# Seven block products for two more pairs of a feed-forward layer, with the input's block sums made two in a slot

## The chip, the cores and the metric

The kernel runs on one core of a Trainium2 chip. Its time is the device time of one execution in microseconds (us). TensorE (PE) does the matmuls, VectorE (DVE) and ScalarE (ACT) the elementwise work, GpSimd (POOL) a little more of it, and SyncE (SP) issues the DMAs. Each engine works through its own queue in order; they meet through semaphores.

## The reference

One transformer block on x of 512 tokens by 1024 features, in float32: a SwiGLU feed-forward, a token mixer (dilated attention and pooling), a second SwiGLU feed-forward and a last RMSNorm, each conditioned by shifts, scales and gates that come from a small vector c through w_ada. What matters here is the first feed-forward:

```python
def swiglu(u, w_in, w_out):
    a, b = jnp.split(u @ w_in, 2, axis=-1)
    return (jax.nn.silu(a) * b) @ w_out

u = modulate(rmsnorm(h, g_norm_ffn1[l]), sh1, sc1)
h = h + 0.5 * gt1 * swiglu(u, w_ffn1_in[l], w_ffn1_out[l])
```

The inner width D_FF is 2816, that is 22 tiles of 128 columns for a and 22 for b.

## The kernel before

**Layout and precision.** Everything is held with features on the 128 partitions and the 512 tokens along the free axis. A float32 product is made of three matmuls of rounded parts (fp32r): high weights by high input, high by low, low by high. So each weight chunk of 128 x 1024 (one DMA of 512 KB into one of three `raw` buffers) is first *split*: ScalarE rounds it into the ring `whi` (L280), VectorE subtracts that from the original into `wlo` (L292). The ring has place for seven chunks. `look(n)` splits the chunks up to n ahead of the one that PE takes next, as far as raw buffers are free, and the place where it is called in the program sets the place of the splits in the queues of ScalarE and VectorE. The normalised input u is held in the same way as UH and UL.

**Pairs and parts.** A pair j is tile j of a and of b; silu(a) * b of it is one 128-row tile of the second matmul's input, kept as high and low parts HI, HK. The 22 tiles are worked in five parts (`PARTS`): input matmuls for some pairs, then the output projection of one part, whose results are added into H, eight tiles of 128 features, by VectorE (L852). Before the projection of part 0 stand pairs 4 and 5 (pairs 0 to 3 belong to the start); before that of part 1 pairs 6 to 9; then four more pairs for each part.

**Plain pairs and duos.** A plain pair (`ffn_pair`) takes two weight chunks and 2 x 24 matmuls with 512 moving columns (L323 to L325). A *duo* does two pairs at once by Strassen's scheme in its form with few additions (Winograd's): the weights of two pairs (halves of the 1024 rows by 256 columns for a and 256 for b) and u (halves of the features by halves of the tokens) are cut into 2 x 2 blocks, and seven products of blocks replace eight. In `duo` they are numbered 0 to 6; each is 24 matmuls with 256 moving columns (`product`, L709 to L711), into three banks in the order A, B, A, C, A, B, A. Since A goes on accumulating, ScalarE must copy it out after products 0, 2 and 4, and the copies stand directly behind them in the program (L716): after product 0 A is copied into bank C, after product 2 into `u2`, after product 4 into `u3`; B is copied into `p5` after product 1.

The seven weight operands, in the order in which they are taken, come from the four loaded blocks r11, r12, r22, r21 as follows (`make`, L228, on VectorE):

```
0: r11        1: x0 = r12 - r11    2: x1 = r22 - x0    3: r21
4: r12 = r22 - r12 (in place)      5: r22              6: x0 = r21 - x1
```

Each is then split like a loaded chunk. x0 and x1 live in two of four big tiles X, which hold the blocks of u (a11, a12, a21, a22) until the sums are made; the other two become additional raw buffers once the first duo has begun.

**The sums of u's blocks** (`u_steps`) are made once: sums S0, S1, S2 on VectorE (L669) with a rounding by ScalarE (L675) and a low part by VectorE (L676), and one last difference whose split (L678, L679) comes behind product 0 of the first duo. These are seven steps in the list `todo`. `ffn` takes one step from it behind each of the eight adds into H in the projection of part 0, and the sums write over a11 and a21, where the weight differences go.

**Order around the change in the old kernel.** Pairs 4 and 5, projection of part 0 (with the sums), pairs 6 and 7 plain, duo 8 (pairs 8 and 9), projection of part 1, two duos, projection, and so on. The second feed-forward has the same parts, with its pairs 0 to 3 plain, and is not touched.

**Conditioning work.** Beside plain pairs and behind the adds into H of parts 1 to 3, `bg` does one step of the product of w_ada with c on VectorE (L346), each with a DMA of 512 KB. 24 such steps are left after part 0 and must be done by the end of part 3's projection.

Of the kernel before, what the change touches and what calls it, by code (L numbers as in the profile page):

```python
# [115 lines left out]

U_AT = (0, 16, 0)

PLAIN = {0: 8, 2: 4}
PARTS = ((0, 4), (4, 8), (8, 12), (12, 16), (16, 22))  # L120
NH = 6

# [14 lines left out]
class Kernel:  # L137
# [6 lines left out]
    def plan(self):  # L144
        (i1, o1), mix, (i2, o2) = chunk_widths()
        self.chunks = []
        for name, ws in (("wf1i", i1), ("wf1o", o1), ("wmix", mix), ("wf2i", i2), ("wf2o", o2)):
            off, rec = 0, []
            for w in ws:
                rec.append((name, off, w))  # L150
                off += P * w
            self.chunks.append(rec)
        f1i, f1o, mx, f2i, f2o = self.chunks


        self.loads, self.order, self.last = [], [], {}

        def plain(recs):
            for r in recs:
                n = len(self.loads)  # L160
                self.loads.append(r)
                self.last[n] = len(self.order)
                self.order.append((r[2], n, ("raw", n), None))

        def blocks(recs):
            n = len(self.loads)
            self.loads.extend(recs)
            r11, r12, r22, r21 = (("raw", n + i) for i in range(4))
            x0, x1 = ("x", 0), ("x", 1)
            for need, src, make in ((0, r11, None), (1, x0, (x0, r12, r11)), (2, x1, (x1, r22, x0)), (3, r21, None),  # L170
                                    (3, r12, (r12, r22, r12)), (3, r22, None), (3, x0, (x0, r21, x1))):
                for j, x in enumerate((r11, r12, r22, r21)):
                    if x == src or (make and x in make):
                        self.last[n + j] = len(self.order)
                self.order.append((D, n + need, src, make))

        def ffn(n, ins, outs, first):
            j, at = first, 0
            if first:
                plain(ins[:KT])  # L180
                at = KT
            for part, (k0, k1) in enumerate(PARTS):
                while j < pairs_before(n, part):
                    if j < PLAIN[n]:
                        plain(ins[at:at + 2])
                        j, at = j + 1, at + 2
                    else:
                        blocks(ins[at:at + 4])
                        j, at = j + 2, at + 4
                plain(outs[part * KT // 2:(part + 1) * KT // 2] if part + 1 < len(PARTS) else outs[-KT:])  # L190

        ffn(0, f1i, f1o, FIRST)
        base = len(self.order)
        plain(mx)
        ffn(2, f2i, f2o, 0)
        self.fetched = self.done = self.made = 0
        self.pos, self.held, self.retired, self.half = 0, None, [], None
        self.at, self.start, self.top = {}, {}, 0
        self.buf = {}
        self.units = {base + i: 2 * P for i in (4, 5)}  # L200
        self.units.update({base + i: T for i in range(16, 20)})
# [55 lines left out]
    def split_hi(self):  # L257

        held = max(self.pos - 1, 0) if self.held is None else self.held
        i = self.done  # L260
        if self.half or i == len(self.order):
            return False
        got = self.room(i, held)
        if got is None:
            assert i >= self.pos, "no room"
            return False
        self.start[i] = self.top
        self.at[i], self.top = got
        self.fetch(i)
        assert self.fetched > self.order[i][1], "no buffer"  # L270
        self.make(i)
        r = self.source(self.order[i][2])
        parts = []
        for o, c in self.at[i]:
            for x in self.pieces(i, self.order[i][0]):
                x = slice(max(x.start, c.start), min(x.stop, c.stop))
                if x.start < x.stop:
                    parts.append((slice(o + x.start - c.start, o + x.stop - c.start), x))
        for y, x in parts:
            self.nc.scalar.activation(self.hi[:, y], r[:, x], AF.Copy)  # L280
        if i + 1 < len(self.order) and self.order[i + 1][3] and self.order[i + 1][1] < self.fetched:
            self.make(i + 1)
        self.half = (r, parts)
        return True
# [529 lines left out]
    def ffn(self, n, j, last=None):  # L814
# [10 lines left out]
        for part, (k0, k1) in enumerate(PARTS):  # L825
            tail = part + 1 == len(PARTS)
            while j < pairs_before(n, part):
                if j < PLAIN[n]:
                    self.ffn_pair(j, beside)
                    j += 1  # L830
                else:
                    self.duo(j, last, tail and j + 2 == FT)
                    last = None
                    j += 2
            if n == 0:
                last = self.beside_out(part) or last
            nk = k1 - k0
            hk = [(self.HH[k % NH], self.HL[k % NH]) for k in range(k0, k1)]
            if not tail:
                for m in range(0, KT, 2):  # L840
                    self.look(4)
                    w = self.take()
                    bs = [self.nb(), self.nb()]

                    for ka, kb in ((0, nk - 1), (nk - 1, nk)) if m == 0 else ():
                        for i in range(2):
                            for k in range(ka, kb):
                                self.mm3(bs[i], *w[nk * i + k], *hk[k], k == 0, k == nk - 1)
                    for i, b in enumerate(bs):
                        for k in range(nk if m else 0):  # L850
                            self.mm3(b, *w[nk * i + k], *hk[k], k == 0, k == nk - 1)
                        v.scalar_tensor_tensor(self.H[m + i], b, gate[:, m + i:m + i + 1], self.H[m + i],  # L852
                                               op0=OP.mult, op1=OP.add)
                        if n == 0 and part:
                            self.bg()
                        if self.todo:
                            self.todo.pop(0)()
                    self.step()
                continue

            def ks(m):
                self.look(max(3, min(m + 2, 5)))
                return [(hi, lo, *hk[k]) for k, (hi, lo) in enumerate(self.take())]

            if n == 2:
                self.sums.close()
                op = self.f2.enter_context(self.tc.tile_pool(name="f2o", bufs=1))
                self.OO = op.tile([P, KT * T], F32, name="out").rearrange("p (m t) -> p m t", m=KT)
                self.O = [self.OO[:, m, :] for m in range(KT)]

            kl = [ks(0), ks(1)]
            bs = [self.nb(), self.nb()]
            for ka, kb in ((0, nk - 2), (nk - 2, nk)):
                for m in range(2):
                    for k in range(ka, kb):
                        self.mm3(bs[m], *kl[m][k], k == 0, k == nk - 1)
            for m in range(3 if n else 4):
                if m > 1:
                    bs.append(self.nb())
                    for k, x in enumerate(ks(m)):  # L880
                        self.mm3(bs[m], *x, k == 0, k == nk - 1)
                v.scalar_tensor_tensor(self.H[m], bs[m], gate[:, m:m + 1], self.H[m], op0=OP.mult, op1=OP.add)
                self.sumsq(m, self.H[m])
                if n == 2:
                    nc.scalar.activation(self.O[m], self.H[m], AF.Copy, scale=self.g(3)[:, m:m + 1])
                for _ in range(6):
                    if self.todo:
                        self.todo.pop(0)()
            if n:
                self.out_end((3, 4, 5, 6, 7), ks, gate)  # L890
            else:
                self.trig_spread()
                self.out_tail((4, 5, 6, 7), ks, gate, 1, lambda m: self.X[0][:, m % 2 * HT:])

    def beside_out(self, part):

        if part == 0:
# [4 lines left out]
            self.bg_fetch()  # L902
            self.sums = self.open_sums()
            self.todo, last = self.u_steps(0)
            return last
        if part == len(PARTS) - 1:
            assert self.ada_next == 48 and not self.adat, self.ada_next
# [637 lines left out]
```

## Time and profile before

| | |
|---|---|
| median of three runs | 1030.19 us (1028.4 to 1030.54) |
| the profiled execution | 1027.69 us, span of its instructions 1025.9 us |
| busy: TensorE, weight load, VectorE, ScalarE | 1010.4, 912.5, 750.4, 435.1 us |
| mean granted TensorE clock | 0.994 |
| HBM read | 135.82 MB |

Busy times are those of the one profiled execution. A matmul's row holds start and duration in the pipeline, so the durations of successive matmuls overlap; how long a stage takes on TensorE is read from the starts. A row in square brackets names what ended the idle time in front of an instruction. Lines (L...) are those of the old kernel; in the new one they are two to seven higher.

### The profile page before, as it was taken

The page shows a single profiled execution, that of the slowest core. Times are in us where ns is not written, and L with a number is a line of the kernel's source. Part 1 is how long each engine was busy: PE and PEld are TensorE (multiplying, and loading weights), DVE is VectorE, ACT ScalarE, POOL GpSimd, SP SyncE. Part 2 cuts the span into 40 slices and gives each one's busy share as a digit, 9 for nine tenths or more (in the row PEclk, how much of TensorE's full clock was granted, in tenths as well). Part 3 has the DMA queues.
Part 4 walks back from the last instruction along what each step waited for, and adds up shares of the span by engine and source line. Part 5 has one row for each costly group of instructions (what it writes and reads, how often), then busy time and mean ns, then how long its engine had stood idle before and what let it go on. Part 6 is the DMA issues. An engine that isn't in the chain of part 4 may idle for free.

```text
span 1025.9 us, 15526 instructions
## 1 busy us (share of the span) xinstructions
PE 1010.4 (98%) x6364; PEld 912.5 (89%) x6364; DVE 750.4 (73%) x1073; ACT 435.1 (42%) x638; POOL 37.7 (4%) x39
## 2 busy tenths in 40 slices
PE   8999999999999899999999999999999999999997
PEld 6888898989999899889988888898899899998997
DVE  7968779789786677779546777467787776676754
ACT  6443253525434452334324333454355344352553
POOL 0000000000000100006200000200000000000011
PEclk9999999999999989999999999999999999999998
DMA  9866456555523323222144774322344224241312
GB/s 337 276 213 226 129 200 206 164 165 168 182 72 117 105 78 100 66 79 77 40 176 164 267 248 141 100 67 64 101 148 140 83 96 152 83 142 45 109 35 83
DMA packets 43113, 139.60 MB, mean 136 GB/s; under 512 B 4897, under 2 KB 8225, under 8 KB 43042
## 3 DMA queue, kind: packets, MB, share of 16 engines
q1 hardware_dynamic: 42034, 137.82, 41.1%
q8 instruction: 50, 0.82, 0.3%
q10 hardware_dynamic: 1008, 0.79, 0.2%
q14 instruction: 21, 0.17, 0.1%
HBM read 135.82 MB, written 2.77 MB: 135 GB/s over the span
## 4 chain that ended last, share of the span: by engine, by line
PE 95%; DVE 2%; ACT 1%; issue 1%; DMA 0%; ACTq 0%; DVEq 0%
PE bank L323 17%; PE bank L324 17%; PE bank L325 17%; PE bank L709 10%; PE bank L711 10%; PE bank L710 10%; PE bank L1475 2%; PE bank L1477 1%; PE bank L1479 1%; PE bank L1074 1%; PE bank L1253 1%; PE bank L1254 1%; PE bank L1255 1%; PE bank L1022 1%; PE bank L1051 1%
## 5 line engine op out<-in xcount | busy, mean ns | idle before, releaser
L292 DVE TENSOR_TENSOR wlo<-raw,whi 128x1024 fp32r<-128x1024 f32 (+2 forms) x151 | 176.9, 1175 | 75.6 <-ACT whi L280 75.3
L280 ACT ACTIVATE whi<-raw 128x1024 fp32r<-128x1024 f32 (+2 forms) x151 | 150.4, 1003 | 41.8 <-DVE raw L228 39.9
L323 PE MATMUL bank<-UH,whi 128*128 128x512 f32 (+1 forms) x432 | 159.0, 368 | 0.0
L324 PE MATMUL bank<-UL,whi 128*128 128x512 f32 (+1 forms) x432 | 154.9, 359 | 0.2 <-DVE UL L451 0.2
L325 PE MATMUL bank<-UH,wlo 128*128 128x512 f32 (+1 forms) x432 | 154.9, 358 | 0.0
L323 PE MATMUL bank<-HI,whi 128*128 128x512 f32 (+1 forms) x406 | 147.6, 364 | 0.0
L324 PE MATMUL bank<-HK,whi 128*128 128x512 f32 (+1 forms) x406 | 147.1, 362 | 0.0
L325 PE MATMUL bank<-HI,wlo 128*128 128x512 f32 (+1 forms) x406 | 147.0, 362 | 0.0
L709 PE MATMUL bank<-UH,whi 128*128 128x256 f32 x512 | 141.6, 277 | 0.0
L710 PE MATMUL bank<-UL,whi 128*128 128x256 f32 x512 | 141.6, 277 | 0.0
L711 PE MATMUL bank<-UH,wlo 128*128 128x256 f32 x512 | 141.6, 277 | 0.0
L292 DVE TENSOR_TENSOR wlo<-X,whi 128x1024 fp32r<-128x1024 f32 (+2 forms) x88 | 104.5, 1189 | 45.8 <-ACT whi L280 45.6
L709 PE MATMUL bank<-SH,whi 128*128 128x256 f32 x384 | 107.0, 279 | 0.0
L711 PE MATMUL bank<-SH,wlo 128*128 128x256 f32 x384 | 106.9, 278 | 0.0
L710 PE MATMUL bank<-SL,whi 128*128 128x256 f32 x384 | 106.9, 278 | 0.0
L280 ACT ACTIVATE whi<-X 128x1024 fp32r<-128x1024 f32 (+2 forms) x88 | 89.1, 1027 | 32.9 <-DVE X L228 28.6
L710 PEld LDWEIGHTS bank<-UL,whi 128*128 128x128 f32 x512 | 96.1, 188 | 0.3
L709 PEld LDWEIGHTS bank<-UH,whi 128*128 128x128 f32 x512 | 96.1, 188 | 0.3
L711 PEld LDWEIGHTS bank<-UH,wlo 128*128 128x128 f32 x512 | 96.3, 188 | 0.0
L325 PEld LDWEIGHTS bank<-UH,wlo 128*128 128x128 f32 x432 | 81.3, 188 | 12.8
L324 PEld LDWEIGHTS bank<-UL,whi 128*128 128x128 f32 x432 | 81.5, 189 | 12.3 <-issue 0.5
L323 PEld LDWEIGHTS bank<-UH,whi 128*128 128x128 f32 x432 | 81.4, 189 | 11.8 <-issue 0.5
(225 smaller groups left out, 1750.4 us busy)
## 6 DMA issues: line engine op xcount, KB each, us to landing
ada<-wada SPq DMA_DIRECT2D x47, 512.0 KB, 5.0
raw<-wmix SPq DMA_DIRECT2D x44, 512.0 KB, 3.6
raw<-wf1i SPq DMA_DIRECT2D x34, 512.0 KB, 4.5
raw<-wf2i SPq DMA_DIRECT2D x30, 512.0 KB, 3.6
X<-wf2i SPq DMA_DIRECT2D x14, 512.0 KB, 3.6
cs<-wada SPq DMA_DIRECT2D x12, 512.0 KB, 3.5
AR<-wada SPq DMA_DIRECT2D x12, 512.0 KB, 4.6
raw<-wf2o SPq DMA_DIRECT2D x12, 512.0 KB, 3.5
```

The lines of the kernel that those rows point to most:

```text
L280: self.nc.scalar.activation(self.hi[:, y], r[:, x], AF.Copy)
L292: self.nc.vector.tensor_tensor(self.lo[:, y], r[:, x], self.hi[:, y], op=OP.subtract)
L323: M(ps, hi, uh, start=start, stop=False)
L324: M(ps, hi, ul, start=False, stop=False)
L325: M(ps, lo, uh, start=False, stop=stop)
L709: M(o, hi, uh, start=start and p == 0 and k == 0, stop=False, skip_group_check=True)
L710: M(o, hi, ul, start=False, stop=False, skip_group_check=True)
L711: M(o, lo, uh, start=False, stop=k == 3, skip_group_check=True)
L1022: M(S[:, o + i * P:o + i * P + P], qz[:, (2 * i + h) * P:(2 * i + h + 1) * P], k[:, toks], start=True, stop=True)
L1051: nc.tensor.transpose(b[:, i * P:i * P + P], p[:, i * P:i * P + P], self.ident)
L1074: M(o, pt[:, blk * P:blk * P + P], v, start=i == 0, stop=i == len(srcs) - 1)
L1475: M(b, hi, self.UH[k], start=k == 0, stop=False)
```

## The change

Pairs 6 and 7 become a duo, in front of duo 8, so that it is now the first one and follows the projection of part 0 directly. During that projection two steps of `todo` are taken behind each add into H, so that the sums are made behind the first four of its eight adds. A flag `ready`, which is set by an eighth entry at the end of the list, keeps `split_hi` from splitting any operand that needs a weight difference before the sums are made. The weights of pairs 6 and 7 are laid out by blocks. The `bg` steps that stood beside the plain pairs 6 and 7 fall to the projections of parts 1 to 3.

```diff
-PLAIN = {0: 8, 2: 4}
+PLAIN = {0: 6, 2: 4}
...
@@ plan
         self.fetched = self.done = self.made = 0
+
+        self.ready = True
...
@@ split_hi
         if self.half or i == len(self.order):
+            return False
+        if self.order[i][3] and not self.ready:
             return False
...
-        if i + 1 < len(self.order) and self.order[i + 1][3] and self.order[i + 1][1] < self.fetched:
+        if i + 1 < len(self.order) and self.order[i + 1][3] and self.ready and self.order[i + 1][1] < self.fetched:
             self.make(i + 1)
...
@@ ffn
                         if n == 0 and part:
                             self.bg()
-                        if self.todo:
-                            self.todo.pop(0)()
+                        for _ in range(2 if not self.ready else 1):
+                            if self.todo:
+                                self.todo.pop(0)()
...
@@ beside_out
             self.todo, last = self.u_steps(0)
+            self.ready = False
+            self.todo.append(lambda: setattr(self, "ready", True))
             return last
```

## The prediction

> **What bounds the kernel now.** I read the page first, then the windows around the change, then the timelines of TensorE, VectorE and ScalarE. On the page, the span, the line of busy engines and the chain of waits:
>
> ```profile
> span 1025.9 us, 15526 instructions
> PE 1010.4 (98%) x6364; PEld 912.5 (89%) x6364; DVE 750.4 (73%) x1073; ACT 435.1 (42%) x638; POOL 37.7 (4%) x39
> PE 95%; DVE 2%; ACT 1%; issue 1%; DMA 0%; ACTq 0%; DVEq 0%
> ```
>
> 95% of the chain that ended last is TensorE (PE). A change gains what it takes from PE's stream and loses any wait that it puts into it, one for one. So two questions decide: how much PE time do seven block products save, and can VectorE (DVE) and ScalarE (ACT) have their operands ready?
>
> The windows show the place. Columns: the stretch, its length, then busy time of PE, weight load, DVE, ACT and POOL, granted clock, DMA share and GB/s. The stretches are pairs 6 and 7 done plainly, the first duo (pairs 8, 9), two later duos, and the part of the output projection after them:
>
> ```profile
> 105.40:127.80 22.40, 22.40 (x98) 17.95 (x97) 16.92 (x21) 6.43 (x8) 0.00 (x0) 1.00 0.42 134
> 127.80:147.00 19.20, 19.20 (x170) 19.20 (x169) 15.74 (x16) 12.31 (x15) 0.00 (x0) 1.00 0.68 230
> 168.70:207.30 38.60, 38.60 (x338) 38.56 (x338) 32.94 (x36) 20.93 (x26) 0.00 (x0) 1.00 0.59 186
> 207.30:229.00 21.70, 21.70 (x98) 17.98 (x97) 18.92 (x26) 5.56 (x6) 0.00 (x0) 1.00 0.50 155
> ```
>
> PE has no idle time in any of them; in duos DVE is some 82 to 85% busy (15.74 of 19.20, 32.94 of 38.60), so it can't make up lost time quickly.
>
> **Part 1: what PE saves.** The timeline of PE gives the borders: the first matmul of the first output projection, that of the plain pairs 6 and 7, the first duo's first matmul, its second and third product, and the output projection that follows. Columns: start in us, duration, engine, line, operation.
>
> ```profile
> 83.55 0.39 PE L323 MATMUL bank<-HI,whi 128*128 128x512 f32 x1
> ...
> 105.36 0.39 PE L323 MATMUL bank<-UH,whi 128*128 128x512 f32 x1
> 127.75 0.28 PE L709 MATMUL bank<-UH,whi 128*128 128x256 f32 x1
> 130.49 0.28 PE L709 MATMUL bank<-SH,whi 128*128 128x256 f32 x1
> 133.35 0.29 PE L709 MATMUL bank<-SH,whi 128*128 128x256 f32 x1
> 146.97 0.39 PE L323 MATMUL bank<-HI,whi 128*128 128x512 f32 x1
> ```
>
> Two plain pairs are 96 matmuls of 512 columns and take 127.75 - 105.36 = 22.39 us. A duo is 7 products of 24 matmuls of 256 columns and takes 146.97 - 127.75 = 19.22 us, 2.74 us for one product (130.49 - 127.75). If nothing waits, the change saves 22.39 - 19.22 = 3.17 us, and that is the most it can save.
>
> **Part 2: what the first duo has to wait for.** In the old kernel the sums of u's blocks are made during the first output projection (83.55 to 105.36 us on PE), one step behind each of its eight adds into H, and the plain pairs 6 and 7 lie between them and the first duo. Now the duo begins at 105.36 at once. VectorE, where the steps are queued, is already late when the projection's adds begin:
>
> ```profile
> 92.68 0.74 DVE L852 SCALAR_TENSOR_TENSOR H<-bank,mod,H 128x512 f32<-128x512 f32 x1
> 93.34 1.21 DVE L669 TENSOR_TENSOR X<-X 128x1024 f32<-128x1024 f32 x1
> 94.47 0.74 DVE L852 SCALAR_TENSOR_TENSOR H<-bank,mod,H 128x512 f32<-128x512 f32 x1
> 95.68 1.23 DVE L676 TENSOR_TENSOR SL<-X,SH 128x1024 fp32r<-128x1024 f32 x1 [0.47 <-ACT SH L675]
> 96.83 1.22 DVE L292 TENSOR_TENSOR wlo<-raw,whi 128x1024 fp32r<-128x1024 f32 x1
> ...
> 110.31 0.75 DVE L852 SCALAR_TENSOR_TENSOR H<-bank,mod,H 128x512 f32<-128x512 f32 x1
> ...
> 112.11 1.23 DVE L228 TENSOR_TENSOR X<-raw,raw 128x1024 f32<-128x1024 f32 x1
> ```
>
> PE finished the projection at 105.36, but the eighth add into H ran at 110.31: a backlog of 5 us. That was harmless, since pairs 6 and 7 need no sums and their weights were split ahead. I take 92.68 as the starting point of the new walk too, because up to that add every queue holds the same instructions in the same order. Behind it the changed program issues on DVE: add H0, sum, low part of S0; add H1, sum, low part of S2; add H2, sum, low part of S1; add H3, last sum; then at once weight difference x0 = r12 - r11, x1 = r22 - x0, the low parts of both, add H4, add H5, difference r12 = r22 - r12, and the rest.
>
> From the rows: an add takes 0.66 us from start to start (92.68 to 93.34), a 1024-wide operation 1.13 to 1.15. A low part must wait for ScalarE to round the sum first; it starts 95.68 - 93.34 = 2.34 us after its sum does. In the old order an add into H lay inside that wait. With two steps in a slot nothing does, so a slot costs 0.66 + 2.34 + 1.15 = 4.15 us against (110.31 - 92.68) / 7 = 2.5 us in the old order. Three slots: 92.68 + 12.45 = 105.13. The fourth, add and last sum, 0.66 + 1.14: 106.93. x0 and x1 each read the result before them, so I give each its full 1.22 and 0.03 of handover: x0 starts at about 107.0, x1 at 108.25. The low part of x0's weights follows at 109.4 (its rounding on ACT runs beside x1) and ends at 110.6; that of x1 starts 2.34 after x1, at 110.6. H4 111.75, H5 112.4, the difference r12 at 113.05, ended at 114.3.
>
> ScalarE's queue now matters. Its rows around the old first duo:
>
> ```profile
> 94.59 1.06 ACT L675 ACTIVATE SH<-X 128x1024 fp32r<-128x1024 f32 x1 [3.27 <-DVE X L669]
> 131.26 1.06 ACT L280 ACTIVATE whi<-raw 128x1024 fp32r<-128x1024 f32 x1 [1.00 <-DVE raw L228]
> 132.23 0.58 ACT L716 ACTIVATE bank<-bank 128x512 f32<-128x512 f32 x1
> 132.75 1.04 ACT L678 ACTIVATE UH<-X 128x1024 fp32r<-128x1024 f32 x1
> ```
>
> The copy of the first product from bank A to bank C (L716, 0.58 us) stands directly behind the rounding of the difference r12 (L280), in the old program and in the new. PE's third product adds into the same bank A, so it can't start before that copy. In the new order: rounding of r12 from 114.35, the copy 0.97 later at 115.3, done at 115.9.
>
> So on PE: product 0 needs no difference, 105.36 to 108.10. Product 1 waits until 110.6 for its low weights (two of its 24 matmuls can go at 109.35) and ends at about 113.2. Product 2 waits for the copy until 115.9. Unhindered it would have started at 105.36 + (133.35 - 127.75) = 110.96, so 4.95 us are lost here. Products 2 and 3 end at 115.9 + 2 x 2.74 = 121.4. Product 4 adds into A again and waits for the copy u2, on ACT behind the rounding of x0 = r21 - x1. That difference is queued on DVE behind H6, H7, the low part of r12 and the low part of S3: 113.05 + 1.14 + 1.14 (low part of r21) + 2 x 0.66 + 2 x 1.14 = 118.9; rounding 1.25 behind its start (94.59 - 93.34), copy 0.97 later and 0.58 long: 121.7. PE loses 0.35 more and ends three further products at 121.75 + 3 x 2.74 = 130.0. The duo of pairs 6 and 7 thus takes 24.6 us against 22.39: **+2.25 us**, that is -3.17 saved and +5.4 of waits (rounded).
>
> Bounds. The difference r21 needs its load: it reuses r11's buffer, so its DMA is issued when x0 has read that, at 108.2.
>
> ```profile
> raw<-wf1i SPq DMA_DIRECT2D x34, 512.0 KB, 4.5
> ```
>
> With the median of 4.5 us it lands at 112.8, its rounding ends at 113.9, ahead of r12's at 114.35. A load up to half a microsecond longer is covered; one of 6 us would add 1.0. On the other side each of my handovers is uncertain by a few hundredths and about fifteen are in the chain; -0.4 us. So this part is between +1.8 and +3.3.
>
> **Part 3: what else moves.** The next duo (pairs 8, 9) starts at 130.0 with DVE ready: its first weights go into r12's buffer, free at about 117.9, and are there 4.5 us later, at 122.4; and after the waits DVE needs 16 us of work for a duo of 19.2, as in the second window. I give it nothing; each microsecond of a late load there would be one of PE's. The four steps of the ada sums (L346) that stood beside pairs 6 and 7 move to the fourth projection, which then has eight. The window 207.30:229.00 is a projection with eight, PE busy throughout and with no wait in duos after it: nothing. The same four 512 KB loads are made, and the two spare buffers are freed 22 us earlier: nothing. The adds into H end at about 116.6 instead of 111; the banks that the duo's first two products write hold H2 and H3, read by 105.8: nothing.
>
> Sum: 1025.9 + 2.25 = 1028.15 us of span, 1027.69 + 2.25 = 1029.9 for the profiled execution. The median of the runs shown lies 2.5 us above that execution (1030.19), so **1032.4**.
>
> **Rivals.** *The clock falls during the stall.* The old trace has one long idle time of PE:
>
> ```profile
> 355.93 0.28 PE L325 MATMUL bank<-HI,wlo 128*128 128x256 f32 x1
> 360.55 0.77 PE L408 MATMUL bank<-ones,AR 128*128 128x1 f32 x3 [4.34 <-DVE AR L517]
> 358.00:358.40 0.40, 0.00 (x0) 0.00 (x0) 0.40 (x2) 0.40 (x1) 0.00 (x0) 0.99 0.54 215
> 358.40:360.00 1.60, 0.00 (x0) 0.00 (x0) 1.60 (x4) 0.54 (x2) 0.00 (x0) 0.50 0.87 274
> 365.00:365.20 0.20, 0.20 (x3) 0.20 (x3) 0.16 (x2) 0.00 (x0) 0.00 (x0) 0.50 0.00 0
> 365.20:365.40 0.20, 0.20 (x3) 0.20 (x3) 0.20 (x1) 0.00 (x0) 0.00 (x0) 0.94 0.00 0
> ```
>
> The granted clock went to 0.50 at 358.4, 2.2 us after the last matmul ended (355.93 + 0.28), and came back at 365.2, 6.8 us later. In the new stall PE idles about 2.7 us (113.2 to 115.9) after 2.3 us of idling around product 1. That is longer than 2.2, so the clock may fall. If it falls and comes back after half of those 6.8 us, 3.4 us run at half rate and cost 1.7; the 0.35 of the later wait vanishes in it: +1.35, 1033.8. With all 6.8 us at half rate it costs 3.2 and the result is 1035.3. Against it: the one row is of a gap of 4.34 us, and nothing in this trace shows what a shorter one does; if the clock falls already during product 1, the wait for the copy hides it.
>
> The Trainium skill, TensorE: Matmul & The Clock Gate, section "HAM oscillation — how this bites in real kernels", asks only that PE not idle for more than about 3.4 us. By that rule the clock holds and the sum stays as it is; the row above, with its fall after 2.2 us, speaks for less margin than that.
>
> *The waits hide and the change is faster.* This decides at one point: when the copy of bank A ends. If DVE did other queued work inside the three waits for ScalarE (1.2 us each, 2.34 - 1.14), x0 would be 3.6 us earlier, the copy would end at 112.3, PE would lose 1.35 and 0.35, and the change would gain 1.5 us: 1028.7; with no wait left 1027.0. The break-even is a copy at 113.7. The queue's order speaks against it: nothing stands between a sum and its low part.
>
> *Smaller stall.* A copy 1 to 2 us earlier than I say, if the backlog at 92.68 is shorter in most executions: +0.3 to +1.2, 1031. *Larger stall*: late loads into the buffers of the second duo hold its first products as well, +4 to +6: 1035.5.
>
> **Chances.** Stall with the clock kept 0.42 (1032.4); clock falls 0.36 (1033.8, up to 1035.3); waits hidden 0.08 (1027.0 to 1028.7); smaller stall 0.08; larger 0.06. The range leaves out the hidden waits and the outer ends of the last and second: 1030.3 to 1035.0. About 0.2%, 2.06 us, is what a measurement of this kernel can tell from no change. My likeliest case of +2.25 lies just past it, so I put a third of it within; with the smaller stall and little of the rest, within 0.2% gets 0.25, faster 0.07, slower 0.68.
>
> **What would show it.** In the new profile PE should show its only new idle time between about 108 and 122 us: some 2.3 us that end with the low part of the weights (wlo), 2.7 us ending with the copy bank<-bank, and a short one ending with a copy to u; the second duo's first matmul at about 130.0 and the second projection's at 149.2. On DVE the sums should be in slots of 4.15 us and the eighth add into H at 116. Granted clock below 1.00 between 113 and 122 would show the first rival. A PE with no gap there, and the second projection before 147, would prove the prediction wrong, as would a new wait after 150 us.

## The result: 0.28% slower, and the profile after

The changed kernel takes 1031.95 us (median of 10 runs, 1030.52 to 1034.15), the old one 1029.09 us in the runs beside it (10 runs, 1027.89 to 1030.95). The ratio is 1.0028, with a 95% interval of 1.0018 to 1.0038: slower by 2.86 us, just past what can be told from no change. The profiled execution took 1031.36 us.

The page of the changed kernel, the same three lines as before:

```profile
span 1029.6 us, 15688 instructions
PE 1010.8 (98%) x6436; PEld 916.5 (89%) x6436; DVE 758.4 (74%) x1079; ACT 439.8 (43%) x643; POOL 37.8 (4%) x39
PE 88%; DVE 6%; ACT 2%; issue 2%; DMA 1%; SPq 0%; ACTq 0%; DVEq 0%
```

PE's share of the chain fell from 95% to 88%, VectorE's rose from 2% to 6% and ScalarE's from 1% to 2%: the end of the kernel now hangs on them for a stretch. In the list of the chain's pieces that stretch runs from 61.3 to 123.5 us, so the lateness reaches back to the plain pairs in front of the first projection. PE's timeline shows where it costs PE time. The rows are the first matmul of the new duo, those that started late (in brackets how long PE sat idle, and for what; the rows at 123.53 and 129.20 started 0.35 and 0.2 us late, too little for a bracket), the first matmul of duo 8, and that of the second projection:

```profile
106.96 0.28 PE L713 MATMUL bank<-UH,whi 128*128 128x256 f32 x1
...
111.01 0.39 PE L713 MATMUL bank<-SH,whi 128*128 128x256 f32 x1 [1.06 <-ACT whi L284]
...
112.31 0.38 PE L715 MATMUL bank<-SH,wlo 128*128 128x256 f32 x1 [0.80 <-DVE wlo L296]
...
117.70 0.39 PE L713 MATMUL bank<-SH,whi 128*128 128x256 f32 x1 [1.00 <-ACT bank L720]
...
123.53 0.39 PE L713 MATMUL bank<-SH,whi 128*128 128x256 f32 x1
...
129.20 0.38 PE L713 MATMUL bank<-UH,whi 128*128 128x256 f32 x1
...
132.04 0.28 PE L713 MATMUL bank<-UH,whi 128*128 128x256 f32 x1
...
151.24 0.39 PE L327 MATMUL bank<-HI,whi 128*128 128x512 f32 x1
```

Everything in front of the duo ran 1.60 us later in this execution than in the old profile (106.96 against 105.36), although every queue holds the same instructions up to the first add into H; the last section tells what the traces show of that. Counted from the first matmul behind the first projection, the new duo takes 132.04 - 106.96 = 25.08 us against 22.39 for the two plain pairs, duo 8 takes 19.20, and the whole stretch to the second projection 151.24 - 106.96 = 44.28 us against 41.61: +2.67. The stages right behind 151.24 have their old length (projection 21.78, two duos 38.52 us). The time scatters in front of the stretch, as said, and behind it: from 230 us to the second feed-forward this execution wins 0.6 us on the old one, and that of e4 below, the same program in that part, loses 1.4. The stretch is free of both, so it is the measure for the experiments below, beside the time; it comes from one execution of each kernel.

VectorE's queue in the same time (start, duration, line, operation; in brackets idle time):

```profile
94.29 0.74 DVE L856 SCALAR_TENSOR_TENSOR H<-bank,mod,H 128x512 f32<-128x512 f32 x1
94.95 1.21 DVE L673 TENSOR_TENSOR X<-X 128x1024 f32<-128x1024 f32 x1
97.29 1.23 DVE L680 TENSOR_TENSOR SL<-X,SH 128x1024 fp32r<-128x1024 f32 x1 [1.13 <-ACT SH L679]
98.43 0.74 DVE L856 SCALAR_TENSOR_TENSOR H<-bank,mod,H 128x512 f32<-128x512 f32 x1
...
108.64 1.22 DVE L230 TENSOR_TENSOR X<-raw,raw 128x1024 f32<-128x1024 f32 x1
...
114.77 1.21 DVE L230 TENSOR_TENSOR raw<-raw,raw 128x1024 f32<-128x1024 f32 x1
...
117.04 1.40 DVE L856 SCALAR_TENSOR_TENSOR H<-bank,mod,H 128x512 f32<-128x512 f32 x2
...
119.49 1.22 DVE L683 TENSOR_TENSOR UL<-X,UH 128x1024 fp32r<-128x1024 f32 x1
...
126.34 1.23 DVE L230 TENSOR_TENSOR X<-X,raw 128x1024 f32<-128x1024 f32 x1 [2.08 <-DMA X<-wf1i]
```

A slot of the sums costs 98.43 - 94.29 = 4.14 us, with 1.13 us in which VectorE only waits for ScalarE. The first weight difference comes at 108.64, when PE has been in the duo for 1.7 us; the difference r12 at 114.77. And ScalarE's:

```profile
113.52 1.06 ACT L284 ACTIVATE whi<-raw 128x1024 fp32r<-128x1024 f32 x1 [1.25 <-DMA raw<-wf1i]
116.10 1.06 ACT L284 ACTIVATE whi<-raw 128x1024 fp32r<-128x1024 f32 x1 [1.52 <-DVE raw L230]
117.06 0.58 ACT L720 ACTIVATE bank<-bank 128x512 f32<-128x512 f32 x1
...
122.90 0.58 ACT L720 ACTIVATE u<-bank 128x512 f32<-128x512 f32 x1
...
128.57 0.58 ACT L720 ACTIVATE u<-bank 128x512 f32<-128x512 f32 x1
```

The copy of bank A (117.06) was possible when product 0 ended at about 109.8; it stood behind the rounding of r12, which waited for VectorE. The load of r21 was not what held it: its rounding (113.52) was done before r12 was made (114.77). PE's rows at 117.70, 123.53 and 129.20 each follow such a copy.

### The profile page after: what moved, and what is told of

It reads as the page before. It is cut to its first block, busy times and chain, and to the rows that moved or that the text cites. A ratio compares the mean times of both kernels' runs of the same rounds, so it can differ in the third digit from the quotient of the medians.

```text
span 1029.6 us, 15688 instructions
## 1 busy us (share of the span) xinstructions
PE 1010.8 (98%) x6436; PEld 916.5 (89%) x6436; DVE 758.4 (74%) x1079; ACT 439.8 (43%) x643; POOL 37.8 (4%) x39
## 4 chain that ended last, share of the span: by engine, by line
PE 88%; DVE 6%; ACT 2%; issue 2%; DMA 1%; SPq 0%; ACTq 0%; DVEq 0%
PE bank L327 15%; PE bank L328 15%; PE bank L329 15%; PE bank L713 10%; PE bank L715 10%; PE bank L714 10%; PE bank L1482 1%; PE bank L1484 1%; PE bank L1486 1%; DVE wlo L296 1%; PE bank L1081 1%; ACT whi L284 1%; PE bank L1260 1%; PE bank L1261 1%; PE bank L1262 1%
## 5 line engine op out<-in xcount | busy, mean ns | idle before, releaser
L327 PE MATMUL bank<-UH,whi 128*128 128x512 f32 (+1 forms) x400 | 146.3, 366 | 0.0
L329 PE MATMUL bank<-UH,wlo 128*128 128x512 f32 (+1 forms) x400 | 142.2, 355 | 0.0
L296 DVE TENSOR_TENSOR wlo<-X,whi 128x1024 fp32r<-128x1024 f32 (+1 forms) x92 | 111.0, 1206 | 37.9 <-ACT whi L284 37.6
L284 ACT ACTIVATE whi<-X 128x1024 fp32r<-128x1024 f32 (+1 forms) x92 | 94.4, 1038 | 40.3 <-DVE X L230 39.5
L713 PEld LDWEIGHTS bank<-UH,whi 128*128 128x128 f32 x544 | 102.1, 188 | 0.4
L715 PEld LDWEIGHTS bank<-UH,wlo 128*128 128x128 f32 x544 | 102.4, 188 | 0.0
L714 PEld LDWEIGHTS bank<-UL,whi 128*128 128x128 f32 x544 | 102.1, 188 | 0.3
L329 PEld LDWEIGHTS bank<-HI,wlo 128*128 128x128 f32 x406 | 77.2, 190 | 11.7
L328 PEld LDWEIGHTS bank<-HK,whi 128*128 128x128 f32 x406 | 77.2, 190 | 11.4
L327 PEld LDWEIGHTS bank<-HI,whi 128*128 128x128 f32 x406 | 77.2, 190 | 11.4
```

The source lines that it names most:

```text
L296: self.nc.vector.tensor_tensor(self.lo[:, y], r[:, x], self.hi[:, y], op=OP.subtract)
L327: M(ps, hi, uh, start=start, stop=False)
L328: M(ps, hi, ul, start=False, stop=False)
L329: M(ps, lo, uh, start=False, stop=stop)
L713: M(o, hi, uh, start=start and p == 0 and k == 0, stop=False, skip_group_check=True)
L714: M(o, hi, ul, start=False, stop=False, skip_group_check=True)
```

## The experiments

The theory: PE's stream is shorter by 3.1 us, and more than that is lost because two queues stand in a bad order behind a VectorE that is late. On VectorE the sums wait for ScalarE with nothing in between and the differences queue behind them; on ScalarE the copies that free the banks queue behind roundings whose input VectorE has not made. Rivals: the two steps in a slot, the loads, the clock. For all kernels, the stretch from the first matmul behind the first projection to the first of the second projection, read from PE's timeline of the one profiled execution as above, and the time (median of 5 to 12 runs):

| kernel | stretch, us | against old | time, us | old beside it, us | ratio, 95% interval |
|---|---|---|---|---|---|
| old | 41.61 | | | | |
| changed | 44.28 | +2.67 | 1031.95 | 1029.09 | 1.0028 (1.0018 to 1.0038) |
| e1, one step a slot | 42.87 | +1.26 | 1029.47 | 1028.44 | 1.0015 (1.0003 to 1.0027) |
| e2, sums interleaved | 40.55 | -1.06 | 1028.23 | 1028.44 | 0.9999 (0.9990 to 1.0007) |
| e3, copies ahead | 41.11 | -0.50 | 1028.62 | 1028.44 | 1.0005 (0.9993 to 1.0018) |
| e4, filler matmuls | 44.36 | +2.75 | 1036.29 | 1028.44 | 1.0070 (1.0058 to 1.0082) |
| e5, less backlog | 40.99 | -0.62 | 1029.63 | 1029.60 | 1.0000 (0.9990 to 1.0010) |
| e6, e2 and e3 together | 38.52 | -3.09 | 1026.24 | 1029.60 | 0.9971 (0.9959 to 0.9984) |

**e1: is it the two steps in a slot?** One part of the change undone:

```diff
-                        for _ in range(2 if not self.ready else 1):
+                        for _ in range(1):
```

> The duo of pairs 6 and 7 stays, but the sums are made one step in a slot as in the old kernel, so the first weight difference stands behind the eighth add into H. Queue theory (the stall is the length of VectorE's queue in front of the copy of bank A and of the copy to u2): x0 starts about 0.6 us later than in the changed kernel (14.95 instead of 14.35 us behind the first add into H), since three adds now lie inside the waits for ScalarE; but no add lies between the differences any more, so the copy of A ends some 0.8 us earlier and the copy to u2 1.6 us earlier. Time 0.7 to 1.3 us below the changed kernel's 1031.95, that is about 1030.9, 1.5 to 2.2 above the old kernel's runs. Rival (two steps in a slot are what gets the sums ready in time): time at least 0.5 us above the changed kernel's.

The timeline of e1, by engine: on VectorE the first add, the first difference and the difference r12, on ScalarE the copy of A, on PE product 2:

```profile
93.21 0.74 DVE L856 SCALAR_TENSOR_TENSOR H<-bank,mod,H 128x512 f32<-128x512 f32 x1
108.11 1.22 DVE L230 TENSOR_TENSOR X<-raw,raw 128x1024 f32<-128x1024 f32 x1
112.91 1.22 DVE L230 TENSOR_TENSOR raw<-raw,raw 128x1024 f32<-128x1024 f32 x1
115.21 0.58 ACT L720 ACTIVATE bank<-bank 128x512 f32<-128x512 f32 x1
115.84 0.39 PE L713 MATMUL bank<-SH,whi 128*128 128x256 f32 x1 [1.18 <-ACT bank L720]
```

x0 comes 14.90 us behind the first add (14.35 in the changed kernel), as expected, and yet the stretch is 1.41 us shorter. Two in a slot make the sums ready 0.55 us sooner and push four adds into H between and behind the differences: that part of the change is a loss by itself. The time gained more than I expected: it lies 1.03 us above the old kernel (interval 0.3 to 2.8) and not 1.5 to 2.2. Its twelve runs spread from 1028.40 to 1033.30 us, the old kernel's beside them from 1027.49 to 1030.88; no profile shows one of the long ones, so what made them long stays open.

**e2: work in the waits for ScalarE.** The rounding is issued right behind its sum, the low part one step later:

```diff
+        if n == 0:
...
+            return [high(0, a22, a21, a22, OP.add), high(2, a21, a11, a21, OP.subtract), low(0, a22),
+                    high(1, a11, a22, a11, OP.subtract), low(2, a21), add(a12, a12, a11, OP.subtract), low(1, a11)], last
```

> As the changed kernel, but the seven steps of the sums are put in another order: sum S0, sum S2, low part of S0, sum S1, low part of S2, last sum, low part of S1, with each rounding on ScalarE right behind its sum, so that VectorE has other work while ScalarE rounds. Queue theory: three waits of 1.2 us go, x0 starts 10.7 instead of 14.35 us behind the first add into H, PE's stalls in the first duo shrink from 5.4 us to about 2 (1.4 at product 2, the rest at the copies to u2 and u3). Time 1.0 to 1.5 us below the old kernel, 3.5 to 4.2 below the changed one. Rival (loads): the stall is set by the load of r21 and by the loads of the second duo and not by VectorE: the gain is under 1.5 us and the time stays above the old kernel's.

The timeline of e2, VectorE, ScalarE and PE:

```profile
93.78 0.74 DVE L868 SCALAR_TENSOR_TENSOR H<-bank,mod,H 128x512 f32<-128x512 f32 x1
94.44 2.48 DVE L695 TENSOR_TENSOR X<-X 128x1024 f32<-128x1024 f32 x2
96.83 0.74 DVE L868 SCALAR_TENSOR_TENSOR H<-bank,mod,H 128x512 f32<-128x512 f32 x1
97.49 1.21 DVE L700 TENSOR_TENSOR SL<-X,SH 128x1024 fp32r<-128x1024 f32 x1
...
104.60 1.23 DVE L230 TENSOR_TENSOR X<-raw,raw 128x1024 f32<-128x1024 f32 x1
113.03 0.58 ACT L732 ACTIVATE bank<-bank 128x512 f32<-128x512 f32 x1
113.66 0.39 PE L725 MATMUL bank<-SH,whi 128*128 128x256 f32 x1 [1.37 <-ACT bank L732]
```

No low part waits any more, x0 comes at 10.82 us behind the first add, and of PE's waits 1.37 at product 2 and a short one at product 4 are left. The stretch is 3.73 us shorter than the changed kernel's, and 2.03 longer than that of e6, which has no wait: the 2 us of stall that I expected. The time fell by 3.1 us against the changed kernel (taken from the two differences to the old one), but less below the old kernel than I expected: -0.2 us, with an interval from -1.0 to +0.7 that holds the stretch's -1.06 only at its edge. By the time alone e2 is not told from the old kernel.

**e3: the copies ahead on ScalarE.** VectorE's order up to the differences is as late as in the changed kernel:

```diff
-            self.look(4)
+            self.look(3 if first else 4)
             self.product(bank, u, start)
```

> As the changed kernel, but in the first duo the splits run three operands ahead instead of four, so that on ScalarE the copy of bank A stands ahead of the rounding of the difference r12, and the copy to u2 ahead of that of x0 = r21 - x1. VectorE's work and the sums stay as late as they are. Queue theory: the copy ends 2.5 us earlier (behind the rounding of r21), product 4 starts about 2.5 us earlier; time 2 to 2.9 us below the changed kernel, near the old kernel's. Rival (only VectorE's lateness counts, the place of the copies does not): no more than 0.5 us below the changed kernel, because product 4 waits for its difference all the same.

The timeline of e3, ScalarE and PE:

```profile
105.45 0.28 PE L713 MATMUL bank<-UH,whi 128*128 128x256 f32 x1
111.99 1.06 ACT L284 ACTIVATE whi<-raw 128x1024 fp32r<-128x1024 f32 x1 [1.21 <-DMA raw<-wf1i]
112.96 0.58 ACT L720 ACTIVATE bank<-bank 128x512 f32<-128x512 f32 x1
...
116.98 0.59 ACT L720 ACTIVATE u<-bank 128x512 f32<-128x512 f32 x1
109.52 0.39 PE L713 MATMUL bank<-SH,whi 128*128 128x256 f32 x1 [1.07 <-ACT whi L284]
110.82 0.39 PE L715 MATMUL bank<-SH,wlo 128*128 128x256 f32 x1 [0.80 <-DVE wlo L296]
146.56 0.39 PE L327 MATMUL bank<-HI,whi 128*128 128x512 f32 x1
```

Product 1's waits are the same (1.07 and 0.80 us), those for the copies are gone, and the stretch is 3.17 us shorter. So the place of a 0.58 us copy in ScalarE's queue was worth nearly as much as the waits that e2 took out of VectorE's order (3.73). The rival, that product 4 waits for its difference all the same, is refuted. The clock stayed at 1.00 in this execution (100 to 130 us), and product 2 no longer waits for a copy behind which a fall could hide; what e3 gains in an execution in which the clock falls isn't shown. Its times spread like e1's, from 1027.52 to 1033.20 us.

**e4: does the clock cost anything?** Matmuls that keep PE busy where it waited:

```diff
+    def filler(self, n):
+        for k in range(n):
+            self.nc.tensor.matmul(self.B[7][:, :HT], self.UH[k % KT][:, :P], self.UH[k % KT][:, :HT], start=True, stop=True)
...
+            if i < 2 and first:
+                self.filler(16)
```

> As the changed kernel, with 16 additional matmuls of 256 columns (1.8 us) into an unused bank behind product 0 and as many behind product 1 of the first duo, in the time in which PE waits. Queue theory: the granted clock stays at 1.00 through the stall, product 2 still waits for the copy of A; in executions in which the clock fell late in the stall it gains up to 1.35 us, in the others nothing: median 0 to 0.7 us below the changed kernel. Rival (most of what was lost beyond the walk is the clock): 1.3 us or more below it.

The row of product 2 in e4, and PE's windows over the stall (the column before the last two is the granted clock) and of the first three duos of the second feed-forward, where `first` is set too and nothing waits:

```profile
116.58 0.39 PE L713 MATMUL bank<-SH,whi 128*128 128x256 f32 x1 [0.59 <-ACT bank L724]
105.80:117.00 11.20, 10.40 (x84) 9.95 (x84) 11.08 (x12) 5.21 (x6) 0.00 (x0) 1.00 0.18 48
746.60:808.80 62.20, 62.20 (x538) 62.18 (x537) 45.66 (x43) 31.98 (x40) 0.00 (x0) 1.00 0.40 133
```

With the clock at 1.00 throughout, product 2 starts 10.74 us behind the duo's first matmul (116.58 - 105.84), as in the changed kernel (117.70 - 106.96), where the clock fell to 0.50; the stretch differs by 0.08 us. The time rose by 5.0 us against the changed kernel because the filler ran a second time in the second feed-forward, where those three duos take 62.2 us against 57.7 in the old kernel; I had overlooked that, so its time says nothing on the clock and only the stretch does.

**e5: take away the backlog.** Less work for VectorE beside pairs 4 and 5: the kernel leaves out four steps of the ada product, so it doesn't compute the block, and only its queues are compared:

```diff
+        if 20 <= self.ada_next < 24:
+            self.adat.pop(self.ada_next)
+        else:
             self.ada_do(self.ada_next)
...
+        v.memset(self.mod[:, 20:24], 0.0)
```

> As the changed kernel, but four of the eight steps of the ada product on VectorE beside pairs 4 and 5 are left out (their loads stay; four columns of the first gate are set to zero), so that VectorE isn't late when the first projection's adds begin. Order of all queues behind that point as in the changed kernel. Queue theory: the first add into H runs about 4 us earlier, when PE has its bank, and with it the sums, the differences and the copies; the stall in front of product 1 goes, 1.1 us remain at product 2 and about 0.5 at the copies to u2 and u3. From the first duo's first matmul to the second projection about 40.1 us (44.28 in the changed kernel, 41.61 for plain pairs and duo in the old one); time about 1.5 us below the old kernel. Rival (the cost lies in the length of the rest of the chain, sums with their waits, and in the loads, not in the backlog): the stretch stays above 42.5 us.

The timeline of e5, ScalarE, VectorE and PE; its first projection began at 87.36 us:

```profile
91.15 1.06 ACT L284 ACTIVATE whi<-raw 128x1024 fp32r<-128x1024 f32 x1 [1.28 <-DMA raw<-wf1i]
93.38 0.75 DVE L859 SCALAR_TENSOR_TENSOR H<-bank,mod,H 128x512 f32<-128x512 f32 x1
116.80 0.39 PE L716 MATMUL bank<-SH,whi 128*128 128x256 f32 x1 [1.80 <-ACT bank L723]
```

The first add stands 6.0 us behind the projection's start instead of 9.1: 3.1 earlier and not 4, because the split of r11 in front of it now waited for r11's load. The stretch followed by 3.29 us; 0.9 short of what I gave it, since 1.80 instead of 1.1 us are left at product 2. The backlog is a third cause, and taking it away alone turns the sign in the stretch. The time doesn't show it: I expected 1.5 us below the old kernel and measured 0.03 above (interval 1.0 below to 1.0 above).

**e6: both orders.** The edits of e2 and e3 in one kernel.

> The two reorderings together: sums interleaved so that VectorE has work while ScalarE rounds, and splits three operands ahead in the first duo so that the copies of bank A stand ahead of later roundings on ScalarE. Queue theory: x0 is ready before product 1 needs it, the copy of A ends before product 1 does, the copies to u2 and u3 before products 3 and 5 do; no wait is left. The stretch from the first duo's first matmul to the second projection takes 38.5 to 38.9 us, two duos without a wait, against 41.61 in the old kernel: 2.7 to 3.1 us faster than the old kernel. Rival (loads for the second duo, or splits that run less far ahead, become the next bound): the stretch stays above 39.5 us and the gain under 2 us.

The timeline of e6, ScalarE's copy and PE's borders:

```profile
109.70 0.58 ACT L732 ACTIVATE bank<-bank 128x512 f32<-128x512 f32 x1
105.63 0.28 PE L725 MATMUL bank<-UH,whi 128*128 128x256 f32 x1
144.15 0.39 PE L327 MATMUL bank<-HI,whi 128*128 128x512 f32 x1
```

The copy ends at 110.28, before product 1 does (at about 111.2), so product 2 finds its bank free; no row of PE in the stretch has a wait, and two duos take 38.52 us, as long as the next two of the old kernel. The kernel is faster than the old one by 3.36 us, 0.29% (interval 0.16 to 0.41%), a little more than the expected 2.7 to 3.1, and by more than that than the changed one: the same duo, with its operands in time. Against the changed kernel the stretch is 5.76 us shorter, less than the 3.73 of e2 and the 3.17 of e3 added up, because the two edits shorten the same stall.

## Why the prediction was right

**The number.** The change was forecast at +2.25 us and came out at +2.86 in the time and +2.67 in the stretch. That 1031.95 lies so near to the forecast 1032.4 is in part luck: the sum stood on the median of three runs, 1030.19, and ten runs gave 1029.09, so a start 1.10 too high met a change 0.61 too low.

**What PE saves.** 3.17 us were expected; e6, which has no wait left, shows 41.61 - 38.52 = 3.09. The rest is that the two duos take 19.26 each on average and not 19.22.

**The walk along the queues.** With the 1.60 us by which this execution started later taken off, x0 was expected at 107.0 and ran at 107.04; the difference r12 at 113.05, measured 113.17; the copy of A at 115.3, measured 115.46; product 2 at 115.9, measured 116.1; product 4 at 121.75, measured 121.93. The duo took 25.08 us, not 24.6: 0.2 from the hundredths up to product 2, 0.2 at product 6, which followed a copy to u3 that stood on ScalarE behind the rounding of the first difference of duo 8, and the rest in hundredths. That difference waited 2.08 us for a load (the row at 126.34 above), and not for the one that I had walked: r11 of duo 8 went into r12's buffer at 119.60, as forecast with the 1.60 us added, and its rounding at 123.38 did not wait. The late one was r12 of duo 8, which goes into a spare tile X. SyncE could issue it only when VectorE had read the last difference of u out of that tile (the row at 119.49):

```profile
120.73 0.80 SPq L214 DMA_DIRECT2D X<-wf1i  x2
```

It was used 5.6 us later. So the term that was off is "the two spare buffers are freed 22 us earlier: nothing": they come free behind a VectorE that is late. It cost duo 8 nothing, but it reached the end of the first duo.

**A slip.** In the first rival the 6.8 us at half rate cost 3.4 and not 3.2 us; its outer end is then 1035.5, and nothing else changes.

**The clock.** The first rival came true in the profiled execution and cost nothing, by the reason that the prediction put against it: the clock fell during product 1, which then ended at about 116.7, still before the copy. e4 shows the same start of product 2 with the clock kept. In an execution in which it falls later it could still cost what was said; no profile here shows one, so that stays open. The median's +2.86 leaves little for it beside the stretch's +2.67, but two of the ten runs took 1033.95 and 1034.15 us.

**The hidden waits.** The second rival's arithmetic (x0 3.6 us earlier, gain 1.5) is e2: x0 came 3.53 us earlier and the stretch gained 1.06 on the old kernel. It was right that the changed program's order doesn't do this.

**What I missed** is that the copies' place on ScalarE could be had apart from VectorE's lateness. I took the chain from VectorE through the rounding to the copy as one; e3 cut it in the middle and got 3.17 us back.

## What to carry to other kernels

When a stage is pulled forward, ask for each engine what is queued ahead of the instructions that free a bank or buffer: here a copy of 0.58 us, ready to run, stood for 7 us behind a rounding whose input was late, and moving it ahead gave back 3.17 us, as much as the seven products save. A step of two engines in turn (sum, rounding, low part) wants other work between its halves; putting two such steps in a slot packs the waits, not the work. And where a change is worth a few us of a thousand, measure the stretch that it touches by the trace, from an instruction that both kernels have in common, beside the total.

## What was not expected of the hardware

The granted clock fell in pauses far shorter than the old trace's 4.34 us. The windows of the changed kernel in the stall:

```profile
112.00:113.00 1.00, 0.69 (x5) 0.69 (x6) 0.95 (x2) 0.27 (x1) 0.00 (x0) 0.91 0.82 324
113.00:114.00 1.00, 1.00 (x7) 1.00 (x7) 1.00 (x2) 0.48 (x1) 0.00 (x0) 0.50 0.00 0
116.00:117.00 1.00, 0.70 (x5) 0.49 (x4) 1.00 (x1) 0.90 (x1) 0.00 (x0) 0.88 0.00 0
```

From the shares in the first and last row it fell at about 112.8 and came back at about 116.2, 3.4 us later. The idle times before were 1.06 and 0.80 us, with two matmuls between them. The Trainium skill, TensorE: Matmul & The Clock Gate, section "HAM oscillation — how this bites in real kernels", which the prediction weighed, asks for no gap over about 3.4 us; here no gap was longer than 1.06, so that rule doesn't hold as a bound. Nor do the pauses alone decide: e3 had the same two, 1.07 and 0.80 us with two matmuls between them, e1 had 1.59, 0.81 and 1.18, and both kept the clock at 1.00 (105 to 120 us). The same page of the Trainium skill, section "What's actually happening", has windows of 3413 ns that run freely; the 3.4 us of the fall agree with that, and so would e1 and e3, if their pauses lay otherwise in such a window. No run here shows where the windows lay.

The clock at the start differs from execution to execution too. Mean clock of the first 20 us, where both kernels run the same program, in the old kernel's profile:

```profile
0.00:20.00 20.00, 16.46 (x81) 12.81 (x82) 12.95 (x31) 13.14 (x19) 0.20 (x4) 1.00 0.90 327
```

and in the changed kernel's, whose first projection began 1.6 us later:

```profile
0.00:20.00 20.00, 16.20 (x73) 12.85 (x74) 11.51 (x28) 13.05 (x19) 0.20 (x4) 0.91 0.87 320
```

That is only a part of the 1.6 us: ScalarE's row for the first norm's r (L1427, in the new kernel L1434) starts at 13.44 us against 12.73, behind a later load of x, while the clock was still at 1.00. Over all the profiles here the first projection began between 83.55 and 87.36 us, and the clock column doesn't order them: e2 has 0.91 too and began at 84.65, and e5, the last at 87.36, has 1.00, although eight small matmuls at its start (out of `cst` and `r`) took 1.91 us against 1.16 in the old kernel. What delayed e5's start no run here shows.
